# Delta-rule projection in groups of 512 weight columns, its norm weights loaded late, and a transfer price by pieces

## The chip, the cores and the metric

The kernel runs on one core of a Trainium2 chip. The metric is the device time of one execution in microseconds (us). All engines of the core work side by side and meet only at semaphores: PE multiplies matrices (PEld loads its stationary operand), DVE is the vector engine, ACT the scalar engine, POOL the GpSimd, and SP issues transfers between HBM and SBUF. Each engine takes its instructions strictly in the order in which the program lists them, so an instruction that waits holds back all that stand behind it on its engine.

## The reference, cut to what matters

The program is two transformer blocks in float32 on 1024 tokens of width 1024. The change touches the first half of the first block, a mixer with two branches that start from one projection:

```python
h = modulate(rmsnorm(x, norm1_w[l]), shift1, scale1)      # shift, scale from silu(c) @ w_ada
proj = h @ w_in[l]                                        # (1024, 1024) @ (1024, 4104)
r_q, r_k, r_v, r_g, d_q, d_k, d_v, d_z, d_a, d_b = jnp.split(proj, cuts, axis=-1)
...
ret = rmsnorm(retention(rotary(r_q), rotary(r_k), r_v)) * silu(r_g)
qkv = silu(causal_dwconv(concat([d_q, d_k, d_v]), conv_w))   # 3 x 512 channels
g   = -exp(a_log) * softplus(d_a + dt_bias)
dn  = gated_delta_rule(l2norm(q), l2norm(k), v, g, sigmoid(d_b))
dn  = rmsnorm(dn, dn_norm_w[l]) * silu(d_z)
mix = concat([ret, dn]) @ w_out[l]
x   = x + gate1 * mix
```

After it come a mixture of 32 experts, a second mixer (neighbourhood attention and gated linear attention) and an MLP.

## The kernel before

**Precision.** A product in float32 is made of three matmuls in a rounded format (`mm3`): both operands are split into a high part (ACT copies it) and a low part (`wsplit` subtracts on DVE or, for every second weight tile while `lo_pool` is 2, on POOL).

**Weights.** `wload` fetches 512 KB of a weight matrix into one of the `wraw` buffers (three in the projections; four more only in the first stage) and splits it into one of `nw` = 5 pairs `whi`, `wlo`. A `wraw` buffer is free again when both parts are made, a pair when the last matmul has read it.

**Two shapes of the same 512 KB.** `chan_block` takes all 1024 rows of 128 columns: 1024 runs of 512 bytes, at a distance of one matrix row, 4104 floats or 16,416 bytes, in `w_in`. It yields 128 output channels by 1024 tokens in two halves, each 24 matmuls into one PSUM bank. `tok_units` takes four pieces of 256 rows by 512 columns: 256 runs of 2048 bytes each. `tok_block` multiplies tokens by such four units.

**The start.** `first_norm` normalizes eight tiles of x (tile 0 to 3, then 4 to 7), transposes them on PE, and streams 16 pieces of `w_ada` through DVE for shift and scale. `xt` has three buffers, so the last tile of x can be fetched only when PE has transposed tile 4. `split` then makes the high and low parts of h: first for tokens 0 to 511 (half 0), then for 512 to 1023 (half 1), which needs all of tiles 4 to 7.

**The delta rule's projection.** `dn_project` runs `chan_block` on twelve groups of 128 columns (k, q, v), with a convolution of four taps on DVE and a SiLU on ACT behind each, and stores them to `qkv_d`. After the first four, `dn_decays` makes the decays; it fetches the eight last columns of `w_in` (`abr`: 1024 runs of 32 bytes). The two PSUM banks of `acc` alternate, and `cr` has two buffers, so half 0 of two channels can run before half 1 of the first.

**Then** `dn_chunks` (chunks of 128 tokens: `dn_pre`, `dn_blocks`, and the serial `dn_scan`), `tok_blocks` (five column blocks: 0, 512, 1024, 1536, 3584) and `retention` are interleaved. `dn_norm_w`, 128 floats, is broadcast to 128 partitions (`dnw`) and halved on DVE at the head of `tok_blocks`; its first use is in the block of column 3584.

**Order.** No order is written out by hand. `Program` records every operation with its buffers, `price` gives it a cost, and `flush` places all of them with a list scheduler: on each engine the ready operation with the longest priced path behind it (`prio`, plus `boost`) goes first. For transfers it keeps one server (`dma_free`) that works them off one by one, each for `op.dma`, and eight in flight (`lanes`). Engines then run in the planned order, whatever the real times are. `hold` puts transfers behind a given transfer in SP's queue. From `first_norm` on, `hold` is the last of the `w_ada` pieces. There are two plans: one from the start through the experts, and one for the rest.

```python
            if name == 'dma_start':
                op.cost, op.lat = 475.0, 930.0
                op.dma = size / 360.0 * (2.0 if run < 512 else 1.0)
```

Here `size` is the transfer's bytes and `run` its longest contiguous run, the smaller of both sides; the unit is ns.

Of the kernel before, what the change touches and what calls it, by code (L numbers as in the profile page):

```python
# [15 lines left out]
AF = mybir.ActivationFunctionType  # L16
OP = mybir.AluOpType
# [4 lines left out]
T = 1024  # L22
# [12 lines left out]
def dsize(dt):  # L35
    return 2 if dt == BF else 4
# [54 lines left out]
def elems(ap):  # L91
    n = 1
    for s, c in ap.ap[1:]:
        n *= c
    return n
# [59 lines left out]
class Program:  # L155
# [202 lines left out]
    def price(self, op, name, out, args, reads, k):  # L358
        n = elems(out)
        psum = out.tensor.name == self.pname or any(r.tensor.name == self.pname for r in reads)  # L360
        ptr = any(elems(r) == 1 for r in reads) and n > 1
        if name in ('dma_start', 'indirect_dma_start'):
            size = 1
            run = 1 << 20
            for ap in [out] + reads[:1]:
                c, last = 1, ap.ap[-1]
                if last[0] == 1:
                    c = last[1]
                run = min(run, c * dsize(ap.dtype))
                size = n * out.ap[0][1] * dsize(out.dtype)  # L370
            if name == 'dma_start':
                op.cost, op.lat = 475.0, 930.0
                op.dma = size / 360.0 * (2.0 if run < 512 else 1.0)
            else:
                op.cost, op.lat, op.dma = 1040.0, 900.0, size / 360.0
        elif op.eng == PE:
            f32 = args[0].dtype == F32
            kk, m = args[0].ap[0][1], elems(args[0])
            if name == 'transpose':
                op.cost = 107.0  # L380
            elif f32:
                op.cost = (n * 1.68 if n >= 127 else 415.0 if m > 64 else 135.0) * (2 if kk < 128 else 1)
            else:
                op.cost = max(n * 0.4166, 107.0) * (2 if kk < 128 else 1)
                if n <= 130 and m > 64:
                    op.cost = 208.0
        elif op.eng == ACT:
            op.cost = 55.0 + n * 0.833 + (40.0 if not psum else 0.0) + (93.0 if 'accum_out' in k else 0.0)
            op.table = TABLES.get(str(args[1]).split('.')[-1])
        elif op.eng == DVE:  # L390
            if name in ('tensor_scalar', 'tensor_copy', 'memset') and not psum:
                op.cost = 69.0 + n * 0.52
            else:
                op.cost = 68.0 + max(n, elems(reads[0])) * 1.042
            op.cost += 61.0 if ptr or psum and name != 'tensor_tensor' else 0.0
        elif name == 'memset':
            op.cost = 40.0 + n * 0.83
        elif 'pow' in str(k.get('op')):
            op.cost = 300.0 + n * 165.0
        else:  # L400
            op.cost = 160.0 + n * 2.0
# [160 lines left out]
class Kern:  # L562
# [117 lines left out]
    def chan_block(self, w, col, m, h, evac):  # L680
# [3 lines left out]
        for half in range(2):  # L684
# [3 lines left out]
                self.mm3(p, wh[:, k], wl[:, k], hi.rhs(s, k), lo.rhs(s, k), k == 0, k == 7)  # L688
            evac(half, slice(512 * half, 512 * half + 512), p)

    def tok_units(self, w, col):
        return [self.wload(w, 256 * s, col, 2, 512) for s in range(4)]

# [174 lines left out]
    def dn_project(self, ca, A, h):  # L868
        nc, ins = self.nc, self.ins
        w_in = ins['w_in'][0]  # L870
        hi, lo = h
        with ExitStack() as ce:
            pe = self.pool('pe', ctx=ce)
            self.lo_pool = 2
            cw = self.t(pe, [48, 128], tag='cw')
            nc.sync.dma_start(cw, ins['conv_w'][0].rearrange("j (c p) -> (j c) p", p=128))
            p = self.ps([128, 48], 'sm')
            nc.tensor.transpose(p, cw, self.ident[:48, :48])
            cwT = self.t(pe, [128, 4, 12], tag='cwT')
            nc.vector.tensor_copy(cwT.rearrange("p j c -> p (j c)"), p)  # L880

            self.qkv_d = self.dt([128, 12, T], 'qkv_d')
            for ch in (4, 5, 6, 7, 0, 1, 2, 3, 8, 9, 10, 11):
                cr = self.t(pe, [128, T + 3], tag='cr', bufs=2)
                nc.gpsimd.memset(cr[:, 0:3], 0.0)

                def ev(half, tok, p):
                    nc.scalar.activation(cr[:, 3 + 512 * half:515 + 512 * half], p, AF.Copy)
                self.chan_block(w_in, 2048 + 128 * ch, 128, h, ev)
                cv = self.t(pe, [128, T], tag='cv', bufs=2)  # L890
                nc.vector.tensor_scalar(cv, cr[:, 0:T], cwT[:, 0, ch:ch + 1], None, op0=OP.mult)
                for j in range(1, 4):
                    nc.vector.scalar_tensor_tensor(cv, cr[:, j:j + T], cwT[:, j, ch:ch + 1], cv,
                                                   op0=OP.mult, op1=OP.add)
                nc.scalar.activation(cv, cv, AF.Silu)
                nc.sync.dma_start(self.qkv_d[:, ch, :], cv)
                if ch == 7:
                    self.dn_decays(pe, ca, A, h)
            self.lo_pool = 0

# [61 lines left out]
    def tok_blocks(self, A, h):  # L962
        nc, ins, pd = self.nc, self.ins, self.pd
        w_in = ins['w_in'][0]
# [3 lines left out]
        def rows():  # L968
            for r, c in ((0, 4), (1, 6), (2, 8), (3, 10)):
                for i in range(2):  # L970
                    yield from self.mod_row(c + i, self.mod_d[r:r + 1, 512 * i:512 * i + 512])
        mods = rows()
        dnw = self.bcast_row(ins['dn_norm_w'][0], 128, 'dnw', pd)
        nc.vector.tensor_scalar(dnw, dnw, 0.5, None, op0=OP.mult)
        self.rq_d, self.rk_d, self.rv_d = [self.dt([T, 512], f'r{n}_d') for n in 'qkv']

        def ev_zg(off, half_w):
# [33 lines left out]
        for col, ev in ((0, ev_qk(A['gq'], self.rq_d)), (512, ev_qk(A['gk'], self.rk_d)), (1024, ev_v),  # L1011
                        (1536, ev_zg(0, None)), (3584, ev_zg(512, dnw))):

            def ev_m(tt, ts, p, ev=ev):
                ev(tt, ts, p)
                next(mods, None)
            self.tok_block(w_in, col, h, ev_m)
        for _ in mods:
            pass
        cm.close()  # L1020
# [1324 lines left out]
```

## Time and profile before

| | us |
|---|---|
| median of 3 runs | 2788.2 |
| lowest and highest | 2787.69 and 2794.82 |
| the profiled execution, its own time | 2788.22 |
| its span, first to last instruction | 2786.4 |

The span is cut into stages roughly so: first norm to 70 us, delta-rule projection to 210, chunks with the token blocks and retention to about 620, output and routing to 800, experts to 1410, second mixer to 2020, MLP to the end. Times in the rows are from the span's start.

### The profile page before, as it was taken

Reading aid. Unit: us, or ns where it says so; the run is one execution under the profiler, and the core shown is the slowest. Engines: PE = TensorE matmul, PEld = TensorE weight load, DVE = VectorE, ACT = ScalarE, POOL = GpSimd, SP = SyncE. Lnnn points to the kernel's source line nnn. Section 1 sums busy time; section 2 is a strip of 40 time slices with the busy share of each in tenths; the row PEclk is TensorE's granted clock in tenths of the full one; section 3 lists DMA queues with packets and bytes.
Section 4 is the critical chain, followed back from the end, with each engine's and each line's share of the span. In section 5 each row is a group of like instructions: output and inputs, shape, how many; then the busy total and the mean of one; then the engine's idle time right before and its main releaser. Section 6 shows DMA issues by size and latency. Waiting matters only on the chain. (4 is left out here: it accounts for less than half of the span.)

```text
span 2786.4 us, 35368 instructions
## 1 busy us (share of the span) xinstructions
PE 2612.6 (94%) x12662; PEld 1996.7 (72%) x12662; DVE 1676.1 (60%) x2585; ACT 1106.3 (40%) x1936; POOL 601.4 (22%) x651
## 2 busy tenths in 40 slices
PE   5999999989969999999969999999999999999998
PEld 4787777977757766453526777777788888888886
DVE  6566856546689888677756433388345444444445
ACT  4325332332237677555635442377232212212122
POOL 3106532323441112322225111343100000000001
PEclk9999999999979999999989999999999999999999
DMA  8446577464359999999977323443211111111111
GB/s 244 88 136 209 178 238 203 141 232 171 143 203 360 322 352 339 360 312 357 326 264 245 113 91 117 125 134 84 87 46 46 54 46 53 38 53 54 46 54 68
DMA packets 325009, 468.84 MB, mean 168 GB/s; under 512 B 70170, under 2 KB 152782, under 8 KB 321758
## 3 DMA queue, kind: packets, MB, share of 16 engines
q1 hardware_dynamic: 318174, 449.76, 49.7%
q0 software_dynamic: 6656, 16.79, 1.8%
q8 instruction: 100, 1.64, 0.2%
q14 instruction: 79, 0.65, 0.1%
HBM read 395.62 MB, written 76.76 MB: 170 GB/s over the span
## 5 line engine op out<-in xcount | busy, mean ns | idle before, releaser
L346 PE MATMUL psum_all<-sbuf 128*128 128x512 f32 (+7 forms) x12662 | 2612.6, 367 | 161.3 <-DVE sbuf L346 94.7
L346 PEld LDWEIGHTS psum_all<-sbuf 128*128 128x128 f32 (+4 forms) x12662 | 1996.7, 176 | 776.8 <-issue 166.9
L346 ACT ACTIVATE sbuf<-sbuf 128x1024 fp32r<-128x1024 f32 (+9 forms) x792 | 708.3, 914 | 808.7 <-PE psum_all L346 535.6
L346 DVE TENSOR_TENSOR sbuf<-sbuf,sbuf 128x1024 fp32r<-128x1024 f32 (+3 forms) x538 | 615.4, 1163 | 272.3 <-ACT sbuf L346 266.6
L346 ACT ACTIVATE sbuf<-psum_all 128x512 f32<-128x512 f32 (+14 forms) x774 | 364.6, 482 | 824.7 <-PE psum_all L346 769.9
L346 POOL TENSOR_TENSOR sbuf<-sbuf 128x512 f32<-128x512 f32 (+9 forms) x301 | 357.4, 1196 | 505.0 <-DVE sbuf L346 349.3
L346 DVE TENSOR_TENSOR sbuf<-sbuf 128x512 f32<-128x512 f32 (+16 forms) x345 | 212.2, 628 | 214.6 <-ACT sbuf L346 168.4
L346 DVE TENSOR_TENSOR sbuf<-sbuf,psum_all 128x512 f32<-128x512 f32 (+3 forms) x327 | 217.6, 673 | 157.0 <-PE psum_all L346 156.9
L346 POOL TENSOR_SCALAR sbuf<-sbuf 128x1 f32<-128x1 f32 (+3 forms) x182 | 81.9, 452 | 1034.3 <-ACT sbuf L346 938.2
L346 DVE TENSOR_TENSOR sbuf<-psum_all,sbuf 128x512 f32<-128x512 f32 (+12 forms) x306 | 182.5, 608 | 153.9 <-ACT sbuf L346 79.0
L346 DVE SCALAR_TENSOR_TENSOR sbuf<-sbuf 128x512 f32<-128x512 f32 (+5 forms) x247 | 200.7, 820 | 56.1 <-POOL sbuf L346 39.8
L346 DVE TENSOR_SCALAR sbuf<-sbuf 128x32 f32<-128x32 f32 (+7 forms) x220 | 108.7, 507 | 50.1 <-ACT sbuf L346 24.1
L1786 POOL DMA_INDIRECT y_d<-sbuf x35 | 57.5, 1642 | 195.7 <-DVE sbuf L346 194.1
L346 DVE SCALAR_TENSOR_TENSOR sbuf<-sbuf,psum_all 128x128 f32<-128x128 f32 (+1 forms) x100 | 38.5, 411 | 88.7 <-PE psum_all L346 55.1
L1774 POOL DMA_INDIRECT sbuf<-h_d,sbuf x35 | 44.7, 1276 | 186.7 <-PE psum_all L346 153.8
L346 DVE SCALAR_TENSOR_TENSOR sbuf<-psum_all,sbuf 128x128 f32<-128x128 f32 (+9 forms) x109 | 62.0, 586 | 38.0 <-PE psum_all L346 37.6
L346 DVE CUSTOM_DVE_ANT_0 sbuf<-psum_all,sbuf 128x512 f32<-128x512 f32 (+2 forms) x80 | 48.1, 613 | 22.0 <-PE psum_all L346 21.3
L346 POOL MEMSET sbuf<- 64x64 f32 (+10 forms) x54 | 16.9, 314 | 188.4 <-DVE sbuf L346 106.3
L346 POOL TENSOR_TENSOR sbuf<-sbuf,sbuf 128x1024 fp32r<-128x1024 f32 x16 | 39.6, 2478 | 59.0 <-ACT sbuf L346 58.1
L346 ACT ACTIVATE sbuf<-psum_all,sbuf 128x128 f32<-128x128 f32 (+1 forms) x72 | 24.6, 404 | 26.7 <-PE psum_all L346 14.8
L346 DVE COPY sbuf<-psum_all 128x512 f32<-128x512 f32 (+9 forms) x31 | 15.2, 491 | 23.0 <-PE psum_all L346 23.0
L346 ACT ACTIVATION_READ_ACCUMULATOR sbuf<-sbuf 128x1 f32 x152 | 28.9, 190 | 0.0
(18 smaller groups left out, 113.7 us busy)
## 6 DMA issues: line engine op xcount, KB each, us to landing
sbuf<-in_w SPq DMA_DIRECT2D x384, 512.0 KB
sbuf<-in_w_ff SPq DMA_DIRECT2D x64, 512.0 KB
sbuf<-in_w_in SPq DMA_DIRECT2D x56, 512.0 KB
sbuf<-in_w_ada SPq DMA_DIRECT2D x48, 512.0 KB
sbuf<-in_x SPq DMA_DIRECT2D x16, 512.0 KB
sbuf<-qkv_d SPq DMA_DIRECT2D x32, 256.0 KB
pre_d<-sbuf SPq DMA_DIRECT2D x8, 1024.0 KB
sbuf<-pre_d SPq DMA_DIRECT2D x8, 1024.0 KB
```

What stands on the lines that cost most here:

```text
L346: op = self.new_op(eng, lambda: real(*a, **k), name, reads, writes)
L1774: return self.prog.real.gpsimd.indirect_dma_start(out=xg, out_offset=None, in_=self.h2_d, in_offset=bass.IndirectOffsetOnAxis(ap=tok, axis=0),
L1786: st = self.prog.real.gpsimd.indirect_dma_start(out=self.y_d, out_offset=bass.IndirectOffsetOnAxis(ap=dest, axis=0), in_=y, in_offset=None ...
```

## The change

There are three edits. The delta rule's weights are fetched as `tok_units`, four units for a group of 512 columns, and a new `chan_group` runs the four channels of 128 and their two halves on them; the twelve channels, their matmuls, splits, convolutions and stores stay as many and as large, in the same order (4 to 7, 0 to 3, 8 to 11). The load and halving of `dn_norm_w` move from the head of `tok_blocks` to the block of column 512, behind the load of its fourth unit (`hold`). And `price` counts a transfer as its number of runs times 5 ns, or times the run's bytes by 360 if that is more: runs of 1800 bytes and over cost what they did, shorter ones more. This last edit holds for every transfer of the program, and so both plans are made anew.

```diff
--- before.py
+++ after.py
@@ -370,7 +370,7 @@
                 size = n * out.ap[0][1] * dsize(out.dtype)
             if name == 'dma_start':
                 op.cost, op.lat = 475.0, 930.0
-                op.dma = size / 360.0 * (2.0 if run < 512 else 1.0)
+                op.dma = size / min(run, size) * max(5.0, min(run, size) / 360.0)
             else:
                 op.cost, op.lat, op.dma = 1040.0, 900.0, size / 360.0
         elif op.eng == PE:
@@ -688,6 +688,20 @@
                 self.mm3(p, wh[:, k], wl[:, k], hi.rhs(s, k), lo.rhs(s, k), k == 0, k == 7)
             evac(half, slice(512 * half, 512 * half + 512), p)
 
+    def chan_group(self, w, col, h):
+
+        hi, lo = h
+        u = self.tok_units(w, col)
+        for c in range(4):
+            m = slice(128 * c, 128 * c + 128)
+            for half in range(2):
+                s = slice(4 * half, 4 * half + 4)
+                p = self.ps([128, 512], 'acc')
+                for k in range(8):
+                    wh, wl = u[k // 2]
+                    self.mm3(p, wh[:, k % 2, m], wl[:, k % 2, m], hi.rhs(s, k), lo.rhs(s, k), k == 0, k == 7)
+                yield c, half, p
+
     def tok_units(self, w, col):
         return [self.wload(w, 256 * s, col, 2, 512) for s in range(4)]
 
@@ -880,21 +894,23 @@
             nc.vector.tensor_copy(cwT.rearrange("p j c -> p (j c)"), p)
 
             self.qkv_d = self.dt([128, 12, T], 'qkv_d')
-            for ch in (4, 5, 6, 7, 0, 1, 2, 3, 8, 9, 10, 11):
-                cr = self.t(pe, [128, T + 3], tag='cr', bufs=2)
-                nc.gpsimd.memset(cr[:, 0:3], 0.0)
-
-                def ev(half, tok, p):
+            for g in (4, 0, 8):
+                for c, half, p in self.chan_group(w_in, 2048 + 128 * g, h):
+                    ch = g + c
+                    if not half:
+                        cr = self.t(pe, [128, T + 3], tag='cr', bufs=2)
+                        nc.gpsimd.memset(cr[:, 0:3], 0.0)
                     nc.scalar.activation(cr[:, 3 + 512 * half:515 + 512 * half], p, AF.Copy)
-                self.chan_block(w_in, 2048 + 128 * ch, 128, h, ev)
-                cv = self.t(pe, [128, T], tag='cv', bufs=2)
-                nc.vector.tensor_scalar(cv, cr[:, 0:T], cwT[:, 0, ch:ch + 1], None, op0=OP.mult)
-                for j in range(1, 4):
-                    nc.vector.scalar_tensor_tensor(cv, cr[:, j:j + T], cwT[:, j, ch:ch + 1], cv,
-                                                   op0=OP.mult, op1=OP.add)
-                nc.scalar.activation(cv, cv, AF.Silu)
-                nc.sync.dma_start(self.qkv_d[:, ch, :], cv)
-                if ch == 7:
+                    if not half:
+                        continue
+                    cv = self.t(pe, [128, T], tag='cv', bufs=2)
+                    nc.vector.tensor_scalar(cv, cr[:, 0:T], cwT[:, 0, ch:ch + 1], None, op0=OP.mult)
+                    for j in range(1, 4):
+                        nc.vector.scalar_tensor_tensor(cv, cr[:, j:j + T], cwT[:, j, ch:ch + 1], cv,
+                                                       op0=OP.mult, op1=OP.add)
+                    nc.scalar.activation(cv, cv, AF.Silu)
+                    nc.sync.dma_start(self.qkv_d[:, ch, :], cv)
+                if g == 4:
                     self.dn_decays(pe, ca, A, h)
             self.lo_pool = 0
 
@@ -970,8 +986,7 @@
                 for i in range(2):
                     yield from self.mod_row(c + i, self.mod_d[r:r + 1, 512 * i:512 * i + 512])
         mods = rows()
-        dnw = self.bcast_row(ins['dn_norm_w'][0], 128, 'dnw', pd)
-        nc.vector.tensor_scalar(dnw, dnw, 0.5, None, op0=OP.mult)
+        dnw = self.t(pd, [128, 128], tag='dnw')
         self.rq_d, self.rk_d, self.rv_d = [self.dt([T, 512], f'r{n}_d') for n in 'qkv']
 
         def ev_zg(off, half_w):
@@ -1014,7 +1029,14 @@
             def ev_m(tt, ts, p, ev=ev):
                 ev(tt, ts, p)
                 next(mods, None)
-            self.tok_block(w_in, col, h, ev_m)
+            units = self.tok_units(w_in, col)
+            if col == 512:
+
+                hold, self.prog.hold = self.prog.hold, self.rawload
+                self.bcast_row(ins['dn_norm_w'][0], 128, 'dnw', pd, dnw)
+                self.prog.hold = hold
+                nc.vector.tensor_scalar(dnw, dnw, 0.5, None, op0=OP.mult)
+            self.tok_block(w_in, col, h, ev_m, units)
         for _ in mods:
             pass
         cm.close()
```

## Rows read from the trace of the kernel before

**Rows 1.** The page, busy time by engine: us, share of the span, instructions.

```profile
PE 2612.6 (94%) x12662; PEld 1996.7 (72%) x12662; DVE 1676.1 (60%) x2585; ACT 1106.3 (40%) x1936; POOL 601.4 (22%) x651
```

**Rows 2.** Stretches: busy us and instructions by engine, granted clock, DMA share, GB/s.

```profile
0.00:70.00 70.00, 35.90 (x140) 28.38 (x141) 47.26 (x88) 33.83 (x55) 24.65 (x28) 0.93 0.88 243
...
80.90:205.00 124.10, 124.10 (x553) 99.47 (x554) 73.15 (x63) 38.92 (x49) 10.61 (x14) 1.00 0.44 114
```

**Rows 3.** Waits from 44 to 62 us: total, times, longest.

```profile
DVE sbuf L346 <- DMA sbuf<-in_dn_norm_w: 11.0, 1, 11.0
...
ACT sbuf L346 <- DMA sbuf<-in_x: 9.4, 1, 9.4
...
PE psum_all L346 <- ACT sbuf L346: 8.5, 1, 8.5
```

**Rows 4.** Timeline of PE: start, us, instructions merged, [idle before, releaser].

```profile
60.40 9.23 PE L346 MATMUL psum_all<-sbuf 128*128 128x128 f32 x34 [8.45 <-ACT sbuf L346]
...
80.90 29.33 PE L346 MATMUL psum_all<-sbuf 128*128 128x512 f32 x128 [1.96 <-ACT sbuf L346]
```

**Rows 5.** Timeline of ACT, same columns.

```profile
4.58 1.06 ACT L346 ACTIVATE sbuf<-sbuf 128x1024 bf16<-128x1024 f32 x1 [2.59 <-DMA sbuf<-in_x]
...
58.72 1.06 ACT L346 ACTIVATE sbuf<-sbuf 128x1024 bf16<-128x1024 f32 x1 [9.41 <-DMA sbuf<-in_x]
...
78.16 0.26 ACT L346 ACTIVATE sbuf<-sbuf 128x64 fp32r<-128x64 f32 x1 [2.84 <-DMA sbuf<-in_w_in]
```

**Rows 6.** Timeline of SP: transfers as they are issued.

```profile
1.17 0.42 SPq L346 DMA_DIRECT2D sbuf<-in_x  x1
...
37.06 2.96 SPq L346 DMA_DIRECT2D sbuf<-in_w_in  x1
40.06 2.91 SPq L346 DMA_DIRECT2D sbuf<-in_dn_norm_w  x1
43.08 3.05 SPq L346 DMA_DIRECT2D sbuf<-in_x  x1
46.23 2.25 SPq L346 DMA_DIRECT2D sbuf<-in_w_in  x1
```

**Rows 7.** Short stretches, columns as in rows 2.

```profile
42.00:52.00 10.00, 9.12 (x35) 7.03 (x35) 4.18 (x9) 5.19 (x8) 7.62 (x4) 1.00 0.86 49
...
60.00:62.00 2.00, 1.60 (x6) 1.50 (x7) 1.97 (x4) 2.00 (x4) 1.32 (x2) 0.50 0.09 26
...
76.00:78.00 2.00, 2.00 (x9) 1.58 (x9) 1.08 (x3) 0.00 (x0) 0.00 (x0) 1.00 0.24 15
...
116.00:118.00 2.00, 2.00 (x10) 1.65 (x10) 0.24 (x1) 1.72 (x3) 0.00 (x0) 1.00 0.96 93
...
388.00:392.00 4.00, 4.00 (x22) 3.34 (x22) 3.55 (x4) 1.82 (x4) 3.62 (x4) 1.00 0.95 270
1474.00:1478.00 4.00, 3.79 (x18) 2.77 (x17) 3.63 (x4) 3.15 (x5) 3.66 (x6) 1.00 1.19 326
```

**Rows 8.** Instructions by form, 100 to 140 us: count, busy us, mean ns, idle before.

```profile
L346 PE MATMUL psum_all<-sbuf 128*128 128x512 f32 x145 | 33.2, 389 | 0.0
...
L346 ACT ACTIVATE sbuf<-sbuf 128x1024 fp32r<-128x1024 f32 x4 | 4.2, 1056 | 8.5 <-PE psum_all L346 8.5
...
L346 DVE TENSOR_TENSOR sbuf<-sbuf,sbuf 128x1024 fp32r<-128x1024 f32 x2 | 2.5, 1226 | 6.5 <-ACT sbuf L346 6.5
...
L346 POOL TENSOR_TENSOR sbuf<-sbuf,sbuf 128x1024 fp32r<-128x1024 f32 x2 | 4.8, 2400 | 17.9 <-ACT sbuf L346 17.9
```

**Rows 9.** Waits of PE from 210 to 600 us, first and last of five.

```profile
PE psum_all L346 <- ACT sbuf L346: 6.8, 4, 2.8
...
PE psum_all L346 <- DMA sbuf<-rq_d: 2.1, 3, 0.8
```

**Rows 10.** Timeline of SP, 590 to 623 us: a store of mix_d, the last of zg_d.

```profile
594.02 0.41 SPq L346 DMA_DIRECT2D mix_d<-sbuf  x1
...
622.15 0.33 SPq L346 DMA_DIRECT2D zg_d<-sbuf  x1
```

## The prediction, made before the changed kernel ran

> **What bounds the kernel now.** I read the page's busy times first. PE is busy for 2612.6 of 2786.4 us [rows 1], so what matters is where PE stands still, and what ends that. Next the stretches: from 0 to 70 us PE has 35.9 us of work, and from 80.9 to 205 it has no gap at all [rows 2]. So the projection itself, which the change rewrites, is PE's own work, and faster transfers inside it are worth nothing. What can be won lies ahead of it. The waits from 44 to 62 us show three that run at once: DVE waits 11.0 us for the norm weights, ACT 9.4 us for a tile of x, and PE 8.5 us for ACT [rows 3]. The timelines give the order. ACT stands still until 58.72 for the last tile of x, and PE, which has to transpose, until 60.40, because the PSUM bank waits behind ACT's stalled instruction [rows 4, 5]. Last comes the reason for the late tile. SP issues it at 43.08, after the third weight piece and the norm weights, and each of these issues holds SP for about 3 us [rows 6]. From 42 to 52 us the transfer engines are 86% busy and move only 49 GB/s [rows 7]. So in this stretch the core waits for transfers that are slow though the engines are busy.
>
> **The weights in 2 KB runs.** Bytes and count stay: twelve pieces of 512 KB. At 16,416 bytes from run to run, the 512-byte runs go at 93 GB/s with the engines 96% busy, and the 2 KB runs of the same matrix at 270 [rows 7]. A piece thus takes 524/270 = 1.9 us in place of 5.6. The three pieces issued ahead of x take some 5.8 us together; in the old form the engines are still busy with such runs up to 52 [rows 7]. By 43.08 hardly anything then stands ahead of the last tile, whose issue time itself stays, since its buffer is freed by PE. The first tile of the program was issued at 1.17 and ACT began on it at 4.58 [rows 5, 6], 3.4 us with a constant ahead of it. With that price the last one lands at 46.5, before ACT has come to it at 58.72 − 9.41 = 49.31. **Gain: all of ACT's 9.4 us.** If it lands at 52 instead, the gain is 6.7.
>
> The Trainium skill ("DMA: Bandwidth & Descriptors", Specifications) names 512 B as enough for line rate. By that the regrouping would save nothing. The trace agrees for the second block's matrix, whose rows are 12,416 bytes long: 326 GB/s from 1474 to 1478 us, in a stretch that carries 512-byte runs [rows 7]. It disagrees for this matrix, at 93. Neither enters the sum, which goes by the rates of this matrix.
>
> **The norm weights.** DVE's wait of 11.0 us is side by side with ACT's, so it adds nothing to the 9.4, but both must go. What DVE does after it (the low parts of h and the scaling of the last tile) is then done by the time that the tile is there. At the new place the load stands in SP's queue behind four 2 KB weight units, whose 270 GB/s are three times the rate of the old queue ahead. Its halving on DVE may wait again, and behind it would stand the evictions of the chunks. I have no row for a wait there, so the bounds are 0 and the old 11.0; I take 0, since the load at the old place waited behind transfers that no longer exist in that shape, and 3 as its upper end in the range, as PE has the token blocks' matmuls to fill in.
>
> **The clock.** After the idle stretch PE is granted 0.50, that is 1.2 of 2.4 GHz, at 60 to 62 us [rows 7]. The work of the next 5 us or so then takes twice as long, which costs about 2.7. Without the idle time it does not fall. But the high and low parts of half 1 on DVE and ACT run alongside, and they release most of PE's next matmuls. I take 1.0, bounds 0 and 2.7.
>
> **The gap at 80.90.** PE waits 1.96 us for ACT [rows 4], which had stood 2.84 us at 78.16 for the 32-byte columns of the decays [rows 5] before it could split the next weight piece. After the change the group's four units are split before, so PE has matmuls that need no new weights. Gain 2.0, bounds 0 and 2.0.
>
> **What it adds at the start.** A psum group now needs four units, not one. Three raw buffers can be filled ahead, and the fourth load can only go when the first unit is split, as the fourth piece does now at 46.23 [rows 6]. With 3.4 us to land, 1.06 on ACT and 1.23 on DVE or 2.40 on POOL [rows 8], the unit is ready at 52 to 53. PE stopped at 60.40 − 8.45 = 51.95 [rows 4] inside the first group. So it waits about a microsecond there, while half 1 is still to come. Cost 1.0, bounds 0 and 2.
>
> **What it adds at the group's edges.** There are five pairs of split buffers and a group holds four; `abw` takes a fifth high part behind the first group. So three or four units of the next group must be split while the last psum group runs. That group lasts 24 x 0.229 = 5.5 us (33.2/145 from [rows 8]), and frees a pair every 1.4 us. The first is free at 1.4, ready at 1.4 + 1.06 + 2.40 = 4.9 even on POOL, and wanted at 5.5. The last is free at 5.5, ready at 7.8 (DVE) or 9.0 (POOL), and wanted at 5.5 + 4.1 = 9.6. It fits, with little to spare when a convolution step stands ahead on DVE. At the first edge the decays' matmuls fill in. Cost for two edges 1.0 in all, bounds 0 and 7 (twice 1.06 + 2.40).
>
> **The new price.** Runs of 2 KB and more keep theirs. The 512-byte loads of chunks and second mixer rise 3.5 times, the 64-byte read of `dn_blocks` from 0.73 to 10.24 us, the decays' columns from 0.18 to 5.12. That is too dear: nearly all of the latter moved between 76 and 78 us with the engines 24% busy [rows 7]. The plan will thus put some consumers later than they need to be and others where they no longer stall. From 210 to 600 us PE's five waits sum to 24.5 us [rows 9], of which the new order can win or lose a part. I take 0, with 8 either way. In the second mixer and the MLP weights are fetched three pieces ahead, so I expect the same time there.
>
> **The sum**, against the profiled execution's 2788.2 (span 2786.4 and 1.8 around it), which equals the median: − 9.4 − 1.0 − 2.0 + 1.0 + 1.0 = − 10.4, so **2777.8 us**. PE has no gap behind 80.9 and the experts start only when the routing is known, so an earlier start of the projection passes through to the end.
>
> **Rivals.**
>
> *The plan goes wrong (slower).* The scans are serial. In the plan each one now has three dearer reads (0.36 to 2.56, and twice 0.73 to 2.56), 5.9 us, and each of the two `dn_blocks` 9.5 us more: 66 us if all stood on the chain. An engine keeps the planned order even if the data is there early, so a part of this becomes real. PE fills with token blocks as long as there are some. A store of `mix_d` at 594.02 that I take for the last scan's, and the last of the gates at 622.15 [rows 10], leave 28 us. The rival decides from there: beyond 28 us of delay PE has nothing to fill with. All 66 would cost 38 − 10 = 28, so 2816; half of the excess costs 19 − 10 = 9, 2797. For it speaks that the price is wrong by several times; against it that most of these reads are fetched ahead. Chance 0.15, at about 2797.
>
> *The transfers stay slow (no change).* If the row distance alone sets the pace, the three units still take until 52, the last tile lands some 3 us sooner (64 KB fewer ahead), and the fourth unit comes at 57 or so. Then 3 is won and as much lost: 2788. Against it speak 270 beside 93 GB/s on one matrix. [...] Chance 0.12.
>
> *The stall moves (no change).* The halving of the norm weights waits 3 us at its new place on the path, and both edges cost their 7: 2777.8 + 3 + 6 = 2787. Chance 0.11.
>
> *The order gets better too (faster).* If half of the 24.5 us goes, 2766. For it speaks that the old plan priced slow transfers too low. Chance 0.12.
>
> **The numbers.** The forecast holds 0.50. A run of this kernel can tell 0.3%, 8.4 us, from no change; 0.04 of the forecast's chance falls short of that. Faster: 0.46 + 0.12 = 0.58. Same: 0.12 + 0.11 + 0.04 = 0.27. Slower: 0.15. The range goes from the better order, 2764, to 2793, which leaves out about half of the slower rival and a tail below; the likeliest case's own is 2770 to 2785.
>
> **What would show it.** Right: no wait of DVE for the norm weights and none of ACT for x between 44 and 62 us; the granted clock at 1.00 through 60; the projection's unbroken PE stretch begins near 70 and ends near 195 and stays unbroken but for a microsecond at an edge; everything behind stands about 10 us earlier. Wrong: x still lands after 52; DVE waits for the norm weights near 330; PE has gaps of several us at two places of the projection; or the stretch from 210 to 620 becomes longer, with PE waiting for DVE or POOL where the scans are alone.

## The result, and the profile after

The changed kernel takes 2868.13 us (median of 6 runs, 2865.93 to 2874.36), the kernel before 2787.94 (6 runs, 2784.0 to 2794.82). The ratio is 1.0287, with a 95% interval of 1.027 to 1.0305: **slower by 80 us**, where 10 us less was forecast. The profiled execution's span is 2865.6 us, its own time 2867.39.

I read the page first, to see whether PE has more work or more idle time.

```profile
PE 2643.8 (92%) x12662; PEld 2021.0 (71%) x12662; DVE 1692.8 (59%) x2585; ACT 1104.3 (39%) x1935; POOL 596.0 (21%) x651
```

The matmuls are as many as before [rows 1]. PE is busy 31 us longer for them and idle 48 us longer (2865.6 − 2643.8 = 221.8, against 173.8). So nothing was added to PE's work: the same instructions stand differently.

**The waits at the start went as forecast, the clock did not.** Stretches of the kernel after, columns as in [rows 2, 7]:

```profile
0.00:70.00 70.00, 38.72 (x140) 29.38 (x141) 55.82 (x96) 36.88 (x60) 25.30 (x30) 0.95 0.73 247
70.00:205.00 135.00, 135.00 (x603) 108.53 (x602) 71.88 (x63) 40.71 (x60) 11.88 (x14) 1.00 0.29 96
42.00:52.00 10.00, 8.62 (x26) 6.00 (x27) 8.56 (x19) 7.48 (x13) 7.25 (x5) 1.00 0.43 122
60.00:62.00 2.00, 0.18 (x1) 0.18 (x1) 2.00 (x5) 1.99 (x5) 0.65 (x1) 0.97 0.01 2
...
62.00:68.00 6.00, 4.06 (x9) 2.88 (x10) 6.00 (x10) 4.58 (x9) 3.57 (x3) 0.50 0.07 5
68.00:70.00 2.00, 2.00 (x9) 1.56 (x9) 1.11 (x2) 0.00 (x0) 0.00 (x0) 0.83 0.04 2
```

Its waits from 44 to 62 us:

```profile
POOL sbuf L346 <- ACT sbuf L346: 7.8, 4, 5.2
...
PE psum_all L346 <- ACT sbuf L346: 2.5, 2, 2.0
...
PE psum_all L346 <- DVE sbuf L346: 1.2, 1, 1.2
```

Its timeline of PE, and after it that of SP:

```profile
57.56 2.29 PE L346 MATMUL psum_all<-sbuf 128*128 128x128 f32 x13 [1.22 <-DVE sbuf L346]
61.82 0.78 PE L346 MATMUL psum_all<-sbuf 128*128 128x512 f32 x1 [1.98 <-ACT sbuf L346]
64.54 10.83 PE L346 MATMUL psum_all<-sbuf 128*128 128x512 f32 x38 [1.94 <-DVE sbuf L346]
```

```profile
37.19 0.38 SPq L346 DMA_DIRECT2D sbuf<-in_w_in  x1
...
44.58 0.33 SPq L346 DMA_DIRECT2D sbuf<-in_x  x1
45.02 9.33 SPq L346 DMA_DIRECT2D sbuf<-in_w_in  x3
```

The three waits of [rows 3] have gone: no engine waits for x or for the norm weights. The last tile of x is issued at 44.58, later than before [rows 6], and still in time; the transfer engines are busy 43% of 42:52 and move 122 GB/s, where they were 86% busy for 49 [rows 7]. Three gaps of 1.2 to 2.0 us stand in place of the 8.45 and 1.96 of [rows 4], and behind the last PE runs without a gap beyond 205. The low clock has not gone, it has moved: it was 0.50 at 60 to 62 us [rows 7], and now it is 0.97 there and 0.50 from 62 to 68, after gaps in which PE had little work.

**Where the 80 us are lost.** Each view of a single buffer gives the first and last start of its transfers. For the kernel after, and then for the one before (of its rows those not yet shown):

```profile
L346 SPq DMA_DIRECT2D sbuf<-nb_d x2: 435/804/1173, 290.9 to 448.9; - x2
...
L346 SPq DMA_DIRECT2D mix_d<-sbuf x16: 319/326/1278, 377.5 to 669.1; - x16
...
L346 SPq DMA_DIRECT2D zg_d<-sbuf x16: 319/332/1725, 400.1 to 544.9; - x16
...
L346 SPq DMA_DIRECT2D sbuf<-rpb_d x32: 573/604/1087, 1754.7 to 1998.0; - x32
```

```profile
L346 SPq DMA_DIRECT2D sbuf<-nb_d x2: 359/362/365, 266.6 to 401.5; - x2
...
L346 SPq DMA_DIRECT2D mix_d<-sbuf x16: 319/320/1409, 343.1 to 617.9; - x16
...
L346 SPq DMA_DIRECT2D sbuf<-rpb_d x32: 573/599/667, 1708.3 to 1929.4; - x32
```

The same reading for two stages more makes a table (us; the right column is the changed kernel with the old price, first experiment below, in an execution of 2786.01 us, 7 above that kernel's median):

| mark | before | after | later by | old price |
|---|---|---|---|---|
| first store of `qkv_d` | 90.5 | 80.4 | −10.1 | 78.5 |
| last store of `qkv_d` | 211.3 | 206.4 | −4.9 | 202.4 |
| last store of `mix_d` | 617.9 | 669.1 | 51.2 | 615.4 |
| second mixer, first read of `x_d` | 1413.0 | 1448.1 | 35.1 | 1405.8 |
| last read of `rpb_d` | 1929.4 | 1998.0 | 68.6 | 1927.7 |
| MLP, first read of its weights | 2022.5 | 2101.7 | 79.2 | 2020.4 |
| span | 2786.4 | 2865.6 | 79.2 | 2784.2 |

So two stages lose: the delta rule's chunks (40 us from the projection's end to the second mixer), and the second mixer (44). Of the second mixer's 44 us, 11 are lost before the heads of attention (the first read of `rpb_d` is 46.4 later, the first of `x_d` 35.1), 22 between the first and the last read of `rpb_d`, and 11 behind them. The MLP takes what it took.

**In the chunks** the last gates are stored at 544.9, where it was 622.15 [rows 10]: the token blocks, PE's filling, are used up 77 us sooner, while the scans come 51 us later. What is left to PE then is retention and the scans. From 490 to 700 us after, and two of these stretches before:

```profile
490.00:560.00 70.00, 66.24 (x471) 60.27 (x468) 46.75 (x90) 27.86 (x75) 29.20 (x28) 1.00 0.53 178
560.00:630.00 70.00, 52.69 (x341) 48.38 (x342) 29.86 (x62) 16.20 (x49) 21.42 (x24) 0.80 0.38 128
630.00:700.00 70.00, 52.63 (x293) 43.66 (x292) 29.75 (x72) 13.99 (x45) 8.78 (x17) 0.83 0.57 184
```

```profile
560.00:630.00 70.00, 61.93 (x377) 54.28 (x375) 33.17 (x59) 24.43 (x66) 19.70 (x21) 0.94 0.71 238
630.00:700.00 70.00, 66.37 (x335) 51.09 (x336) 44.98 (x116) 16.68 (x36) 21.95 (x32) 0.98 0.45 158
```

PE is busy 23 us less in the last 140 us. The granted clock goes down to 0.80 as a mean, so for a part of the time to the lower of its two levels, 1.2 GHz; over the whole span it is 0.969 where it was 0.979, and by an estimate from these two numbers that makes 27 of the 31 us for which the same matmuls keep PE busy longer. When it fell, PE worked in pieces of some microseconds with gaps between them, and one gap near the end is long (timeline of PE, after, then a line of SP's and one of SP's waits, 620 to 665 us):

```profile
563.10 1.62 PE L346 MATMUL psum_all<-sbuf 128*128 128x128 f32 x8 [4.26 <-POOL sbuf L346]
565.41 2.07 PE L346 MATMUL psum_all<-sbuf 128*128 128x128 f32 x8 [0.69 <-ACT sbuf L346]
568.35 2.90 PE L346 MATMUL psum_all<-sbuf 128*128 128x128 f32 x12 [0.87 <-DVE sbuf L346]
...
653.88 1.09 PE L346 MATMUL psum_all<-sbuf 128*128 128x128 f32 x4 [13.39 <-DMA sbuf<-rq_d]
```

```profile
650.00 0.32 SPq L346 DMA_DIRECT2D sbuf<-rq_d  x1
```

```profile
SPq L346 <- DMA mix_d<-sbuf: 6.6, 2, 6.4
```

The long gap is a true wait for a transfer. SP stands 6.4 us for a store of `mix_d` and only then comes to the read of `rq_d`. It does not decide the loss: k4_qkv_read below has waits for `rq_d` of 17.6 us from 550 to 700 us, and loses nothing.

**How a price becomes a stall.** The 64-byte read of `nb_d` shows it. The plan now takes it to last 10.24 us. It is issued at 290.94. From 292 to 294 us the trace has its packets (page of that stretch, after):

```profile
DMA packets 2128, 0.26 MB, mean 131 GB/s; under 512 B 2067, under 2 KB 2067, under 8 KB 2127
```

131 KB in 64-byte runs are 2048 runs, so all of them go in about 2 us. DVE, though, comes to `dn_blocks` much later (timeline, after):

```profile
295.53 1.28 DVE L346 TENSOR_TENSOR sbuf<-sbuf 128x256 f32<-128x256 f32 x2 [0.63 <-POOL sbuf L346]
308.67 0.48 DVE L346 TENSOR_SCALAR sbuf<-sbuf 128x512 f32<-128x512 f32 x1 [11.86 <-PE psum_all L346]
...
309.86 2.28 DVE L346 TENSOR_TENSOR sbuf<-sbuf 128x15 f32<-128x15 f32 x8
```

Since the plan had the data come late, it put work for a modulation row ahead of `dn_blocks`. That work waits 11.86 us for PE, and `dn_blocks`, the last group here, starts at 309.86, 18.9 us after the read was issued. Before, it was issued at 266.59, and DVE's first piece of 15 columns came in this group, at 273.93, 7.3 us later:

```profile
273.07 3.37 DVE L346 TENSOR_TENSOR sbuf<-sbuf 128x256 f32<-128x256 f32 x12 [0.63 <-POOL sbuf L346]
```

No wait names this transfer: it has long landed, and it is only planned late.

The old plan is not free of the opposite fault. From issue to use such a read takes longer than its packets move: before, the second one is issued at 401.5, and DVE goes on at 408.60, 7.1 us later, after a wait of 10.70 us (timeline of DVE, before):

```profile
408.60 3.60 DVE L346 TENSOR_TENSOR sbuf<-sbuf 128x15 f32<-128x15 f32 x15 [10.70 <-DMA sbuf<-nb_d]
```

**In the second mixer** eight heads of attention each read two bias tables twice from `rpb_d` (256-byte runs, new price 2 x 4.48 + 2 x 2.56 us) and one piece of `va_d` (5.12): 19.2 us in the planner's one server, where the old price gave 2 x 1.27 + 2 x 0.73 + 1.46 = 5.5. In SP's timeline of before, the reads of `va_d` stand 18.75 us apart (1850.60, 1869.36, 1888.11, 1906.85), and PE is busy all of that time:

```profile
1850.00:1945.00 95.00, 95.00 (x671) 75.30 (x669) 77.57 (x182) 72.70 (x163) 39.63 (x64) 1.00 0.39 95
```

These five transfers alone are thus priced above the time that PE takes for a head: in the plan the transfers bound a stage that PE bounds on the chip. After:

```profile
1897.00:1921.00 24.00, 24.00 (x171) 19.16 (x171) 21.68 (x49) 19.27 (x42) 11.71 (x19) 1.00 0.69 161
1921.00:1944.00 23.00, 19.18 (x122) 15.26 (x120) 14.53 (x37) 14.00 (x32) 4.28 (x12) 0.93 0.43 90
1944.00:1968.00 24.00, 17.87 (x100) 14.38 (x101) 14.68 (x33) 10.19 (x26) 6.94 (x14) 0.79 0.25 55
1968.00:1998.00 30.00, 26.02 (x167) 19.97 (x165) 19.11 (x41) 18.59 (x42) 10.78 (x16) 0.94 0.34 86
```

The waits there, 1897 to 1998 us, show no transfer either, but long single ones between engines:

```profile
POOL sbuf L346 <- DVE sbuf L346: 46.8, 27, 13.4
DVE sbuf L346 <- ACT sbuf L346: 26.6, 12, 7.0
...
POOL sbuf L346 <- ACT sbuf L346: 19.5, 4, 14.9
```

Before, from 1850 to 1945, the first of these had about the same total, in pieces of at most 3.8 us:

```profile
POOL sbuf L346 <- DVE sbuf L346: 44.5, 23, 3.8
```

### The profile page after: what moved, and what is told of

It is laid out like the page before. It is cut to its first block, busy times and chain, and to the rows that moved or that the text cites. A ratio compares the mean times of both kernels' runs of the same rounds, so it can differ in the third digit from the quotient of the medians.

```text
span 2865.6 us, 35316 instructions
## 1 busy us (share of the span) xinstructions
PE 2643.8 (92%) x12662; PEld 2021.0 (71%) x12662; DVE 1692.8 (59%) x2585; ACT 1104.3 (39%) x1935; POOL 596.0 (21%) x651
## 5 line engine op out<-in xcount | busy, mean ns | idle before, releaser
L346 PE MATMUL psum_all<-sbuf 128*128 128x512 f32 (+6 forms) x12662 | 2643.8, 369 | 209.3 <-DVE sbuf L346 125.1
L346 PEld LDWEIGHTS psum_all<-sbuf 128*128 128x128 f32 (+4 forms) x12662 | 2021.0, 178 | 831.7 <-issue 174.9
L346 DVE TENSOR_TENSOR sbuf<-sbuf,sbuf 128x1024 fp32r<-128x1024 f32 (+3 forms) x538 | 630.5, 1192 | 286.0 <-ACT sbuf L346 274.4
L346 DVE TENSOR_TENSOR sbuf<-sbuf 128x512 f32<-128x512 f32 (+13 forms) x345 | 217.1, 647 | 179.0 <-ACT sbuf L346 163.3
L346 POOL TENSOR_SCALAR sbuf<-sbuf 128x1 f32<-128x1 f32 (+3 forms) x182 | 70.6, 388 | 1122.7 <-ACT sbuf L346 995.2
L346 DVE TENSOR_TENSOR sbuf<-psum_all,sbuf 128x512 fp32r<-128x512 f32 (+13 forms) x306 | 182.0, 607 | 195.0 <-ACT sbuf L346 115.0
L346 DVE CUSTOM_DVE_ANT_0 sbuf<-psum_all,sbuf 128x512 f32<-128x512 f32 (+2 forms) x80 | 48.2, 610 | 18.9 <-PE psum_all L346 18.3
```

The lines of the kernel that those rows point to most:

```text
L346: op = self.new_op(eng, lambda: real(*a, **k), name, reads, writes)
```

## The experiments

Ratios are to the kernel before on the same chip, in brackets the 95% interval. Where a loss in us is given, it is the difference of two ratios times 2788, by their intervals good to 5 to 7 us. Each median lies in one of the ranges named before its run, or within some 2 us of one; in the last run it is the rival's.

**The parts of the change.** Theory: the price alone loses. Rival: the groups or the moved load do.

```diff
 e1_old_price: after, with
-                op.dma = size / min(run, size) * max(5.0, min(run, size) / 360.0)
+                op.dma = size / 360.0 * (2.0 if run < 512 else 1.0)
 e2_price_only: before, with the reverse
 h1_groups_only: before, with chan_group alone
 h2_late_only: before, with the load of dn_norm_w moved alone
```

> The changed kernel with the transfer price put back (groups of 512 columns and late norm weights stay). Theory A, the new price spoils both plans: the 36 us lost by the first plan and the 44 lost by the second are gone and the start's gain is left, 2770 to 2782; the last store of mix_d stands near 610 and not at 669. Theory B, the groups of four units take the chunk stage its overlap and the price does nothing: the first place stays late, 2820 to 2870, with the last store of mix_d near 660.

> The kernel before with nothing but the new price. Theory A: as slow as the changed kernel or slower by the start's gain that it lacks, 2865 to 2885. Theory B: 2780 to 2800.

> The kernel before with the groups of 512 columns alone (old price, norm weights early). By the prediction's steps both waits of the start must go: with the norm weights early DVE still waits for them, but behind 2 KB runs, so the wait shrinks from 11 us to a few: 2778 to 2783. Rival, the norm weights are slow by themselves (128 reads of one row): DVE still waits 8 us or more and the time is 2786 to 2792.

> The kernel before with the norm weights late alone (old price, 128-column weights). By the prediction's steps DVE is free but ACT still waits for the last tile of x behind the slow 512-byte runs: 2784 to 2790. Rival, the norm weights are what clogs the queue: the tile lands by 48 us and the time is 2776 to 2782.

| | median us | ratio |
|---|---|---|
| e1_old_price | 2778.84 | 0.9959 [0.9945, 0.9974] |
| e2_price_only | 2862.98 | 1.0255 [1.0231, 1.0279] |
| h1_groups_only | 2777.58 | 0.9967 [0.9955, 0.9979] |
| h2_late_only | 2789.48 | 1.0005 [0.9996, 1.0014] |

The theory holds: the price alone makes the loss, and without it the change gains 0.41%, 11 us. The groups alone give 0.33%, 9 us. A new plan by itself can move this kernel by as much (last experiment), so the firmer sign of the start's gain is in the waits: in h1_groups_only no engine waits for x or for the norm weights from 44 to 62 us. The moved load gives nothing: without it, behind 2 KB runs, the norm weights hold nobody up, and moved away from 512-byte runs they still leave x waiting (waits of h2_late_only, 44 to 62 us):

```profile
ACT sbuf L346 <- DMA sbuf<-in_x: 7.8, 1, 7.8
```

With the old price e1 keeps 8.9 us at the projection's end (202.4 against 211.3); the changed kernel has 4.9 there.

**Which plan, which runs.** From here on, the base is e1: groups, late load, old price, ratio 0.9959. Each kernel has the new price only where a condition C holds; `plan` counts the calls of `flush`.

```diff
-                op.dma = size / min(run, size) * max(5.0, min(run, size) / 360.0)
+                op.dma = (size / min(run, size) * max(5.0, min(run, size) / 360.0)) if C else size / 360.0 * (2.0 if run < 512 else 1.0)
 e3_price_first_plan:  C = plan == 0
 e4_price_second_plan: C = plan == 1
 f1_first_512up:  C = plan == 0 and run >= 512
 f2_first_short:  C = plan == 0 and run < 512
 g1_second_short: C = plan == 1 and run < 512 and size < 1000000
 g2_second_rpbwrite: C = plan == 1 and run < 512 and size >= 1000000
 g3_second_512up: C = plan == 1 and run >= 512
```

> The changed kernel with the new price in the first plan only (start to the experts), the old price in the second (second mixer and MLP). Theory A: the 36 us lost in the chunk stage stay, the 44 lost in the second mixer go: 2818 to 2832. Theory B, or a second mixer that is late for another reason (what the first plan leaves behind in the queues): 2860 to 2875.

> The changed kernel with the old price in the first plan and the new one in the second only. Theory A: 2814 to 2828, with the chunk stage as in the run with the old price throughout. Theory B: the chunk stage late as in the changed kernel and the second mixer as before, 2815 to 2830 too, but with the last store of mix_d near 660.

> Groups and late norm weights; in the first plan the new price for runs of 512 bytes and more (so the chunk loads from qkv_d and the stores to nb_d rise 3.5 times), the old one for shorter runs and in the whole second plan. Theory A1, the 512-byte loads ahead of each chunk stretch the plan (8 chunks some 5 us each): most of the first plan's 45 us, 2808 to 2825. Theory A2, the short runs of dn_blocks and of the scans do it (9.5 us twice and 2.2 us eight times): 2776 to 2790.

> The complement in the first plan: new price only for runs under 512 bytes (the read of dn_blocks, xb_d, the decays' columns, the router's weights). Theory A1: 2778 to 2795. Theory A2: 2808 to 2825.

> Groups and late norm weights, old price in the first plan; in the second plan the new price only for runs under 512 bytes without the one big store of rpb_d (so the bias tables and values of the eight attention heads, 19 us of priced transfer a head where PE takes 18.7). Theory B1, the heads are planned as bound by transfers and their overlap is lost: most of the second plan's 48 us, 2805 to 2827. Theory B2, the weight loads in 512-byte runs ahead of them are to blame: 2778 to 2790.

> Groups and late norm weights, old price everywhere but for one transfer of the second plan: the 1.9 MB store of rpb_d in 256-byte runs, 10.9 to 38.4 us. If the rest of the second plan's 48 us hangs on this one, which stops the planner's only server for 38 us, 2790 to 2815; if not, 2776 to 2784.

> The complement in the second plan: new price only for runs of 512 bytes and more (weight loads of 128 columns in the second mixer and MLP, 1.46 to 5.12 us). Theory B1: 2778 to 2790. Theory B2: 2800 to 2827.

| | median us | ratio | above the base, us |
|---|---|---|---|
| e3_price_first_plan | 2824.29 | 1.0115 [1.0093, 1.0137] | 43 |
| f1_first_512up | 2809.96 | 1.0076 [1.0056, 1.0095] | 33 |
| f2_first_short | 2790.19 | 0.9996 [0.998, 1.0012] | 10 |
| e4_price_second_plan | 2826.68 | 1.0129 [1.0107, 1.0152] | 47 |
| g1_second_short | 2811.39 | 1.0077 [1.0053, 1.0102] | 33 |
| g3_second_512up | 2787.72 | 0.9991 [0.9977, 1.0006] | 9 |
| g2_second_rpbwrite | 2774.91 | 0.9961 [0.9946, 0.9975] | 1 |

The plans share the loss about evenly and add up: 43 + 47 = 90, against 91 for both (1.0287 − 0.9959). Within each, one class of runs carries most: the 512-byte runs in the first plan (theory A1), the short ones in the second (B1). The 9 and 10 us of the other two are no more than a new plan can make by itself. The store of `rpb_d`, whose price rises most (38.4 in place of 10.9 us), costs nothing; why was not followed up.

**Server or priority.** A price enters twice: into the server that sets when a transfer lands, and into `prio`.

```diff
+                po = size / 360.0 * (2.0 if run < 512 else 1.0)
+                pn = size / min(run, size) * max(5.0, min(run, size) / 360.0)
 k1_server_only:
+                op.dma, op.pdma = pn, po
 k2_prio_only:
+                op.dma, op.pdma = po, pn
 both:
-            op.prio = op.cost + op.dma + op.lat + best
+            op.prio = op.cost + (op.dma if op.pdma is None else op.pdma) + op.lat + best
```

> The changed kernel, but the new price counts only in the planner's server, which sets when a transfer is planned to land; the priorities of all operations are worked out with the old price. Theory A (the planned landing times place the consumers late, and the engines keep that order): most of the loss stays, 2840 to 2875 us. Theory B (the longer priced paths raise the priority of the wrong work): 2770 to 2795 us. Where both carry a part, 2800 to 2840.

> The reverse: the new price only in the priorities, the server with the old one. Theory A: no loss, 2770 to 2795 us, as with the old price and the groups (2778.8). Theory B: 2840 to 2875.

The server alone gives the whole loss: 2875.27 us, 1.0301 [1.0284, 1.0319]. The priorities alone lose nothing to before: 2788.09, 0.9974 [0.996, 0.9987]. So the loss comes through the planned landing times (theory A), not through the priorities.

**Which transfers.** The two reads of `nb_d`, the 32 reads of `qkv_d`, the 8 stores of `nb_d` in the first plan, and the 32 reads of `rpb_d` in the second, each alone, by the same edit:

```diff
 k3_nb_read:   C = plan == 0 and the source is nb_d
 k4_qkv_read:  C = plan == 0 and the source is qkv_d
 l1_nb_store:  C = plan == 0 and the target is nb_d
 k6_bias_read: C = plan == 1 and the source is rpb_d
```

> Groups of 512 and late norm weights; the old price everywhere but for the two reads of nb_d in 64-byte runs, which the first plan takes to last 10.24 us each in place of 0.73. The trace of the changed kernel shows DVE doing a planned-ahead operation that waits 11.9 us for PE while that data is there. Theory that these two reads carry a part of the first plan's loss: 2784 to 2800 us. Rival, that the plan has other work to put there: 2771 to 2783.

> The same base; only the 32 reads of qkv_d in 512-byte runs have the new price in the first plan, 2.56 us each in place of 0.73. In the first plan the runs of 512 bytes and over cost 31 us more than the base. Theory that the loads of the chunks carry that: 2800 to 2815 us. Rival, that the stores of retention's and the experts' buffers with such runs do, or that no single sort of transfer does: 2772 to 2792.

> Groups of 512 and late norm weights; the old price everywhere but for the eight stores of nb_d in 512-byte runs in the first plan, 2.56 us each in place of 0.73. The reads of qkv_d alone lost nothing, and these stores are the only other large transfers with runs of 512 to 1800 bytes in the first plan. Theory that the stores carry its 31 us: 2800 to 2815 us, with the first store of xb_d near 326 us. Rival, that it takes both together, a server that falls behind: 2772 to 2792, with that store near 290.

> Groups of 512 and late norm weights; the old price everywhere but for the 32 reads of rpb_d in 256-byte runs in the second plan (4.48 us in place of 1.27, and 2.56 in place of 0.73). In the second plan the short runs without the store of rpb_d cost 33 us more than the base, and these reads and the eight of va_d (5.12 in place of 1.46) are the large ones among them. Per head the server then works 16 to 17 us in place of 6 to 7, still under PE's 18.7. Theory that a server planned slower than PE is what loses: little or no loss, 2772 to 2792. Rival, that the late reads of the bias alone carry it: 2800 to 2815.

| | median us | ratio | above the base, us |
|---|---|---|---|
| k3_nb_read | 2790.68 | 0.9996 [0.9986, 1.0005] | 10 |
| k4_qkv_read | 2776.63 | 0.9952 [0.9935, 0.997] | −2 |
| l1_nb_store | 2774.45 | 0.9941 [0.9924, 0.9959] | −5 |
| k6_bias_read | 2789.06 | 0.9991 [0.9979, 1.0002] | 9 |

By the ranges named before, k3 and k6 bear out their theory, k4 and l1 their rival. The reads and the stores of f1, taken apart, lose nothing, and together 33 us. The first store of `xb_d`, the sign named for l1, stands at 293.2 there and at 326.2 in f1. So no single sort of these transfers is to blame for the 33. The last store of `mix_d` and the first read of `x_d` in the views of these buffers, against the base's 615.4 and 1405.8, show how a delay of the scans comes through. (Six kernels have the base's first plan: e1, e4, g1, g2, g3 and k6. In their profiles the two marks lie between 609.9 and 617.7 and between 1400.6 and 1407.7, so a mark is good to some 4 us either way.)

| | `mix_d` | later by | `x_d` | later by |
|---|---|---|---|---|
| l1_nb_store | 620.5 | 5.1 | 1398.1 | −7.7 |
| k4_qkv_read | 625.6 | 10.2 | 1403.0 | −2.8 |
| k3_nb_read | 635.1 | 19.7 | 1415.2 | 9.4 |
| f2_first_short | 639.9 | 24.5 | 1417.0 | 11.2 |
| f1_first_512up | 656.7 | 41.3 | 1436.1 | 30.3 |
| e3_price_first_plan | 669.8 | 54.4 | 1450.5 | 44.7 |

What comes through is the delay less 10 to 13 us, whether it is 5 or 54. That these 10 to 13 are slack is not shown: slack would leave l1 where the base is, and it is 7.7 earlier. In the base the last gates are stored after the last scan (616.1 against 615.4), in these six before it, so less is left to do behind the scans.

In the second plan the bias tables alone (14.1 us a head in the server, and 1.5 for `va_d` at its old price, under PE's 18.75) leave the heads at their pace, and g1's short runs do not. Views of `rpb_d`, of k6_bias_read and then of g1_second_short:

```profile
L347 SPq DMA_DIRECT2D sbuf<-rpb_d x32: 573/605/1954, 1699.3 to 1923.3; - x32
```

```profile
L347 SPq DMA_DIRECT2D sbuf<-rpb_d x32: 573/604/1217, 1701.8 to 1944.3; - x32
```

From first to last it is 224.0 us in the one (223.7 in the base) and 242.5 in the other. That fits a server that falls behind PE only when `va_d` is dear as well; `va_d` alone was not tried, and no run stands between 15.5 and 19.2 us a head. The rest of both losses lies behind the heads: from the last read of `rpb_d` to the MLP's first read of its weights g1 takes 103.8 us and k6 99.9, the base 92.7.

**A lower price by pieces.** Half a nanosecond a run, and 430 bytes a nanosecond: my estimate from the transfers' packets in the traces. It does not hold for the 512-byte runs of `w_in` (93 GB/s [rows 7] is 5.5 ns a run), which the groups no longer have.

```diff
-                op.dma = size / min(run, size) * max(5.0, min(run, size) / 360.0)
+                op.dma = size / min(run, size) * (0.5 + min(run, size) / 430.0)
```

> Groups and late norm weights with a price fitted to the traces: 0.5 ns a run and a ns for 430 bytes (512-byte runs 1.69, 2 KB 5.26, 8 KB 19.5 ns). If the new price failed because it is too dear, this one plans as well as the old or better: 2768 to 2782. If any price by pieces reorders the stages for the worse, 2790 to 2860.

It took 2797.95 us, 1.0035 [1.0022, 1.0048], 21 us above the old price: a miss for the theory, and inside the range of the rival, that any price by pieces reorders the stages for the worse. So the new price loses 91 us, but a lower one by pieces does not plan better than the old either. The last store of `mix_d` stands at 628.6, 13.2 later than in the base, so its loss too begins in the first plan; which transfer begins it was not followed up. Eight kernels with the groups and only a part of the prices changed, or all by little (e1, g2, l1, k4, k2, g3, k6 and this one), lie between 0.9941 and 1.0035, 26 us apart. So a new plan by itself can move this kernel by 10 us and more, and of the losses above only those of 33 us and over stand clear of it.

The version that beats both kernels is the groups with the old price, 0.9959 to 0.9967. l1_nb_store's 0.9941 is the lowest, but its interval overlaps theirs, and it would be luck of the plan. The gain itself, 9 to 11 us, is no larger than what a new plan can make.

## Why the prediction was wrong

**The step that failed** is the new price: "I take 0, with 8 either way", and "In the second mixer and the MLP … I expect the same time there". It measured +43 (first plan) and +47 (second). The term was mis-sized, and for half of it the place was not looked at: I had worked out that prices rise 3.5 times in the second mixer, and then asked only whether the weights come early enough there, when the planner's server was what had to be summed up: 19.2 us a head against PE's 18.75. That this sum is what makes the second plan's loss is argued from g1 and k6, not shown. In the first plan it would not have told: f1's dear transfers sum to 40 x 2.56 = 102 us in a stage of some 400, and the loss came through the serial scans.

**The rival that came true** is "the plan goes wrong", with a chance of 0.15 at 2797. Its mechanism was right for the first plan: planned landings late, scans late by 51 us of the 66 at most, PE out of token blocks. One of the signs of being wrong came too: from 560 to 700 us PE waits 9.1 us for POOL, before 0.5. Its 66 us count 16 of the 32 reads of `qkv_d` and no store of `nb_d`, and its slack was wrong. I took 28 us from a store of `mix_d` at 594.02 that I held for the last [rows 10]; the view of the buffer has the last one at 617.9, 4 us before the last gates. In the runs a delay comes through less 10 to 13. It was also limited to the first plan, so its ceiling of 2816 left the second out.

**The start**, − 10.4 forecast: e1 measures − 11.4 and h1 − 9.2. The total came near, by terms that were off both ways.

- ACT's 9.4 us went, as forecast, since the three pieces ahead of x no longer hold the queue. But PE, which bounds, stood still for 8.45 us only [rows 4]. By the Trainium skill ("DMA: Bandwidth & Descriptors", Specifications) 512-byte runs would already have gone at line rate, and the regrouping would have won nothing. The 93 beside 270 GB/s [rows 7], and the wait that went with the longer runs, speak against it for rows 16,416 bytes apart.
- The gap at 80.90 went too, 1.96 us.
- Four units at the start: 1.0 was taken, bounds 0 to 2, while the three gaps sum to 5.1 us (the gaps of this stretch are 3.9 in e1 and 3.0 in h1). They name DVE and ACT, and whether the fourth unit makes them was not tried.
- The clock: 1.0 was taken, since "Without the idle time it does not fall". It fell, at 62 us. Counted as in the prediction, half of the work done at 0.50, it costs 2.4 us after (of 4.06 us from 62 to 68, and a third of the next 2) and 2.7 before, so 0.3 is won.
- The group's edges: 1.0 taken, 0 measured, PE has no gap there.

By these terms the changed kernel wins 8.45 + 1.96 − 5.1 + 0.3 = 5.6 us, and its projection ends 4.9 earlier, not 10. In e1 the projection ends 8.9 earlier; that its whole time came out 11.4 lower may be luck in part, as a new plan can make as much.

**The norm weights**: no wait at the new place, right. That their move is needed ("both must go") was wrong by h1: once the runs ahead are 2 KB, it can stay.

## What to carry to other kernels

Where a list scheduler fixes the order by priced transfers, a price that is too high is not on the safe side: the consumers are planned late, and other work, with waits of its own, is put ahead of data that has long landed. In a stage of like transfers, sum up the planner's server (price times count, here in a head) and compare it with the bound engine's time: at 15.5 us a head against 18.75 the heads kept their pace, at 19.2 they did not. For a serial chain that sum does not tell: look at how much later each link is planned to land. For the slack of such a chain, read the first and last start in the buffer's view, not one row of a window. And where a new plan by itself moves the time by 10 us, a gain of 10 us needs a second sign, such as a wait that is gone.

## What the runs showed of the hardware

- 2048 runs of 64 bytes moved in about 2 us with 16 engines, a fifth of what 5 ns a run gives (10.24). From issue to use another such read took 7.1 us.
- A wait of ACT for a tile of x hung on the shape of other transfers ahead of it: removing a 64 KB load from among 512-byte runs left 7.8 of 9.4 us, making those runs 2 KB long left none.
- In stretches of short pieces with gaps, the granted clock fell to 0.80 as a mean (560 to 630 us); over the span it was 0.969 in place of 0.979, and PE's busy time rose 31 us for the same 12662 matmuls.
- After gaps of 1.2 and 2.0 us with 2.3 us of work between them, the granted clock was 0.50 from 62 to 68 us.
